# RWKV scan terms in four quarters of the PE array, and head sums in four column groups

## The chip, the cores and the metric

One core of a Trainium2 chip runs the whole kernel. The metric is device time in microseconds (us), the median of three runs. Everything is float32; matmuls are done either on float32 operands or on float32r operands, for which a value is split into a high and a low part and three products are summed.

## The reference, cut to what matters

The layer normalises and modulates 256 context and 2048 latent tokens of width 1024, projects them once, and feeds two groups of 8 heads of 64 channels: neighbourhood attention and a bidirectional RWKV-7 scan. Then come the output projection, a LayerNorm and a squared-ReLU MLP. The change touches the RWKV part alone:

```python
kk = split_heads(k * k_k, RW_HEADS)
kk = kk / jnp.maximum(jnp.sqrt(jnp.sum(jnp.square(kk), axis=-1, keepdims=True)), 1e-12)
kd = k[:, :, None] * (1 + (a - 1) * k_a)
...
s_kk = jnp.einsum('bhij,bhj->bhi', S, kk_t)
S = (S * w_t[:, :, None, :] - s_kk[..., None] * (kk_t * a_t)[:, :, None, :]
     + v_t[..., None] * k_t[:, :, None, :])
...
yn = _normalize(y, GN_EPS).reshape(B, T, RW_WIDTH) * gn_g + gn_b
```

So there are two sums over the 64 channels of a head, one of squared keys (for `kk`) and one of squared outputs (for `yn`). The scan is done in chunks of 64 tokens; inside a chunk it needs a 64x64 product of decayed keys with keys for each head, direction and chunk.

## The kernel before, in words

The instructions of each engine are put in order at build time: a scheduler walks the traced program, gives each engine the earliest instruction of the program whose inputs and buffers are ready by its own estimate, and fills gaps with later ones that are ready. The buffers of a tag are handed out in the order of the program.

**Phase 1** (about the first 1005 us) goes over three blocks of 768 tokens in 27 jobs each: the weight column block is loaded and split, `project` (L450) runs 24 matmuls into a PSUM bank, ScalarE copies the bank out (L453) and the job's own work follows. After each half of a job `side` runs one item of deferred work: the key norm, the scan terms, the transposes of values (`nav`, L726), and steps of the triangular solves.

`knorm` (L556) makes the key norm, in two halves of 384 tokens. For each of the four blocks `p` of 128 channels (two heads) it squares the keys (L564) and sums the channels of each head with a float32 matmul (L565) whose weights `hsel` have 8 columns; the four matmuls add into the same 8 rows of a PSUM bank. Square root, maximum and reciprocal follow on 8 rows, and `inv` holds the high part in rows 0 to 7 and the low part in rows 32 to 39 of a tile of 40 rows. `r1a` (L597) spreads it over 128 channels with a float32r matmul of 40 rows (L611).

`r1b` (L667) runs for each of 9 groups of 256 tokens and 4 channel blocks, 36 batches in all. It holds the 16 products of keys (L686): two directions `d`, four chunks `c`, two heads `hd`. Each takes 64 rows and 64 columns of the array, and head 0 uses the upper rows and left columns, head 1 the lower rows and right columns. All 16 go to one bank of the pool `psC`, which has two buffers that `nav`, the layer norm's transposes (L415) and the bonus matmul (L693) use too. One ScalarE copy (L688) and two DMA issues on ScalarE's queue (L690) write the products to the scratch `LB`, which the solves read (L733 on).

**The output stage** (about 1745 to 2090 us) runs beside the last eight steps of the scan's chain. For each 256 tokens `scales` (L1224) does for the outputs what `knorm` does for the keys (L1231 to L1238, tiles of the tag `hm`), and `readout` (L1240) loads `bo` and `gt` on SyncE's queue (L1247, L1249), spreads the scales (L1251) and multiplies. The output projection is L1346.

The chain's own products (`chain_pre`, L1141 and L1145; `chain_main`, L1173 and L1188) are not touched; they serve below as a pattern. L1141 uses the two quarters off the diagonal with 128 moving columns, L1145 the two on it with 64 columns, and they write two different banks.

Of the kernel before, what the change touches and what calls it, by code (L numbers as in the profile page):

```python
# [8 lines left out]
F32 = mybir.dt.float32  # L9
# [52 lines left out]
class Kern:  # L62
# [223 lines left out]
    def p1consts(self, k1):  # L286
# [23 lines left out]
        self.hsel = k1.tile([128, 4, 8], F32, name="hsel")  # L310
# [3 lines left out]
        self.hbc = k1.tile([40, 4, 128], F32R, name="hbc")  # L314
# [241 lines left out]
    def knorm(self):  # L556
        nc = self.nc
        inv = self.inv
        for h in range(2):
            s = slice(h * 384, h * 384 + 384)  # L560
            ps = self.psB.tile([128, 512], F32, name="psb")
            for p in range(4):
# [104 lines left out]
    def r1b(self, sb, p, t, v, cell):  # L667
# [556 lines left out]
    def scales(self, i):  # L1224
# [3 lines left out]
        psv = self.psO.tile([128, 512], F32, name="ops")[:, :256]  # L1228
        for p in range(4):
            sq = P.tile([128, 256], F32, tag="hm", name="ysq")  # L1230
            nc.scalar.activation(sq, y[:, p], AF.Square)  # L1231
            nc.tensor.matmul(psv[0:8], lhsT=self.hsel[:, p, :], rhs=sq, start=(p == 0), stop=(p == 3))
        x = P.tile([8, 256], F32, name="yinv", bufs=1)
        inv = self.inv[i % 2]
        nc.scalar.activation(x, psv[0:8], AF.Sqrt, scale=1.0 / 64, bias=self.eps[0:8, 1:2])
        nc.vector.reciprocal(x, x)
        nc.vector.tensor_copy(inv[0:8], x)
        nc.vector.tensor_tensor(inv[32:40], x, f32(inv[0:8]), ALU.subtract)  # L1238
# [23 lines left out]
    def out_init(self, es):  # L1262
# [9 lines left out]
        self.hsel = o1.tile([128, 4, 8], F32, name="hsel2")  # L1272
        nc.sync.dma_start(self.hsel, a["hsel"])
        hb = self.o2.tile([40, 4, 128], F32, tag="xres", name="hb2")
        nc.sync.dma_start(hb, a["hbc"])
        self.hbc = o1.tile([40, 4, 128], F32R, name="hbc2")
        nc.scalar.copy(self.hbc, hb)
        self.inv = [o1.tile([40, 256], F32R, name="inv%d" % i) for i in range(2)]
        for x in self.inv:
            nc.gpsimd.memset(f32(x), 0.0)  # L1280
# [579 lines left out]
def host(inputs):  # L1860
    I = {k: np.asarray(v) for k, v in inputs.items()}
    o = {}
# [70 lines left out]
```

## Time and profile before

| what | us |
|---|---|
| median of 3 runs | 3413.09 |
| lowest and highest run | 3408.29, 3415.94 |
| profiled execution, its own time | 3414.7 |
| its span | 3412.9 |

The profiled execution is one run of its own: 1.6 us over the median, and 1.8 us longer than the span that the trace covers. A fp32 matmul appears as two records (weights of a first and a second pass), a float32r one as one record; ends of matmuls are modelled, so the time that one takes on the engine is read from start to start.

### The profile page before, as it was taken

What the parts mean: (1) busy time and instruction counts of PE and PEld (TensorE: products, weight loads), DVE (VectorE), ACT (ScalarE), POOL (GpSimd) and SP (SyncE); (2) the same over time, 40 slices, a digit from 0 to 9 for tenths busy, and PEclk for the clock granted to TensorE, in tenths of its full rate; (3) what the DMA queues carried; (4) which work ended last, traced back from release to release, by engine and by line L of the source; (5) the groups of instructions that cost most, each with busy time, mean ns of one, the idle gap of its engine ahead of it and who ended that gap; (6) DMA issues with size and microseconds to landing.
All of it is one profiled execution on the core that took longest, in us unless ns stands there. A gap on an engine that the chain in (4) does not pass through costs nothing.

```text
span 3412.9 us, 65231 instructions
## 1 busy us (share of the span) xinstructions
PE 3192.8 (94%) x25176; PEld 2602.5 (76%) x25176; DVE 2599.1 (76%) x4907; ACT 1523.7 (45%) x2891; POOL 511.0 (15%) x535
## 2 busy tenths in 40 slices
PE   7999899899988899899979989999999989999998
PEld 3888888889876677677667767777788868888886
DVE  5567977888788778767768878866766657899778
ACT  4555465456535455454432124343433343337333
POOL 0000000000005454545343321000000000010001
PEclk9999999999989999999989989999999989999999
DMA  7487366826675655455374546666644455445441
GB/s 259 119 244 213 95 170 167 223 71 178 174 201 145 144 140 126 122 133 128 101 199 150 175 152 224 210 198 206 210 150 148 145 206 162 154 161 203 146 160 69
DMA packets 765338, 561.67 MB, mean 165 GB/s; under 512 B 380412, under 2 KB 653564, under 8 KB 763620
## 3 DMA queue, kind: packets, MB, share of 16 engines
q1 hardware_dynamic: 691738, 523.14, 52.0%
q10 hardware_dynamic: 73290, 34.37, 3.5%
q8 instruction: 198, 3.24, 0.4%
q14 instruction: 112, 0.92, 0.1%
HBM read 359.70 MB, written 197.66 MB: 163 GB/s over the span
## 4 chain that ended last, share of the span: by engine, by line
PE 65%; DVE 14%; DMA 11%; SPq 3%; issue 3%; ACT 2%; POOL 1%; ACTq 0%; DVEq 0%; POOLq 0%
PE psm L450 14%; PE psa L1530 8%; PE psqb L1728 7%; PE psqa L1728 7%; PE psb L1530 4%; PE ops L1346 4%; PE pse L1530 2%; PE psv L1051 2%; DMA ks<-AR 1%; PE psm L468 1%; DMA w<-in_mlp_w 1%; PE pst L1022 1%; PE psg L1141 1%; PE psl L986 1%; PE psd L117 1%
## 5 line engine op out<-in xcount | busy, mean ns | idle before, releaser
L450 PE MATMUL psm<-xh,wh 128*128 128x386 f32 (+1 forms) x1104 | 378.4, 345 | 17.4 <-DVE xh L420 9.5
L450 PE MATMUL psm<-xl,wh 128*128 128x386 f32 (+1 forms) x1104 | 378.8, 343 | 3.1 <-DVE xl L421 3.1
L450 PE MATMUL psm<-xh,wl 128*128 128x386 f32 (+1 forms) x1104 | 376.6, 341 | 0.0
L450 PEld LDWEIGHTS psm<-xh,wh 128*128 128x128 f32 x1104 | 209.2, 190 | 44.8 <-ACT row L453 15.1
L450 PEld LDWEIGHTS psm<-xl,wh 128*128 128x128 f32 x1104 | 209.5, 190 | 16.0 <-issue 8.0
L450 PEld LDWEIGHTS psm<-xh,wl 128*128 128x128 f32 x1104 | 208.8, 189 | 6.1 <-issue 4.1
L1530 PE MATMUL psa<-xh,w1h 128*128 128x512 f32 x512 | 203.9, 399 | 5.1 <-DVE p L1556 4.6
L1794 POOL TENSOR_TENSOR acc<-acc,g 128x1024 f32<-128x1024 f32 x8 | 28.9, 3641 | 1178.2 <-DVE acc L1737 1178.2
L1530 PE MATMUL psa<-xh,w1l 128*128 128x512 f32 x512 | 201.7, 394 | 2.5 <-DVE w1l L1461 2.5
L1530 PE MATMUL psa<-xl,w1h 128*128 128x512 f32 x512 | 202.3, 395 | 0.0
L1678 ACT CAST ah<-al 128x1024 fp32r<-128x1024 f32 x98 | 103.0, 1051 | 213.2 <-DMA al<-HU 205.1
L760 DVE TENSOR_TENSOR stmp<-mp,xp 128x1 f32<-128x1 f32 (+30 forms) x310 | 175.4, 566 | 22.7 <-DMA mp<-LB 10.3
L1679 DVE TENSOR_TENSOR al<-al,ah 128x1024 fp32r<-128x1024 f32 x98 | 121.3, 1237 | 86.0 <-ACT ah L1678 85.9
L436 DVE TENSOR_TENSOR wl<-wst,wh 128x1024 fp32r<-128x1024 f32 x81 | 98.8, 1220 | 98.5 <-ACT wh L435 85.8
L1461 ACT CAST w1h<-w1s 128x512 fp32r<-128x512 f32 x96 | 59.6, 621 | 226.4 <-DVE w1s L1450 87.4
L1728 PE MATMUL psqa<-uh,ah 128*128 128x512 f32 x400 | 155.8, 393 | 3.7 <-ACT uh L1634 3.2
L1728 PE MATMUL psqa<-ul,ah 128*128 128x512 f32 x400 | 157.4, 394 | 0.0
L1728 PE MATMUL psqa<-uh,al 128*128 128x512 f32 x400 | 157.0, 392 | 0.0
L1728 PE MATMUL psqb<-uh,ah 128*128 128x512 f32 x384 | 149.7, 393 | 7.5 <-ACT uh L1634 7.5
L761 DVE TENSOR_REDUCE xp<-stmp 128x1 f32<-128x1 f32 (+30 forms) x310 | 153.9, 497 | 3.1
L1728 PE MATMUL psqb<-ul,ah 128*128 128x512 f32 x384 | 151.0, 393 | 0.0
L1728 PE MATMUL psqb<-uh,al 128*128 128x512 f32 x384 | 150.6, 392 | 0.0
(393 smaller groups left out, 8816.2 us busy)
## 6 DMA issues: line engine op xcount, KB each, us to landing
al<-HU SPq DMA_DIRECT2D x106, 512.0 KB
wst<-in_w_in SPq DMA_DIRECT2D x81, 512.0 KB
w<-in_mlp_w SPq DMA_DIRECT2D x32, 1024.0 KB
wp<-in_mlp_w SPq DMA_DIRECT2D x32, 1024.0 KB
wmod<-in_w_mod SPq DMA_DIRECT2D x48, 512.0 KB
HU<-p SPq DMA_DIRECT2D x96, 256.0 KB
HU<-s SPq DMA_DIRECT2D x84, 256.0 KB
bkc<-BK SPq DMA_DIRECT2D x36, 512.0 KB
```

Source lines behind the costliest of these rows:

```text
L117: self.nc.tensor.matmul(acc[32 * j:32 * j + n, :], lhsT=self.sil[:, k, 0:n], rhs=w, start=(k == 0), stop=(k == 7))
L436: nc.vector.tensor_tensor(wl, w, f32(wh), ALU.subtract)
L450: nc.tensor.matmul(ps[:, :y - x], lhsT=s[:, k, :], rhs=m[:, k, x:y], start=(i == 0), stop=(i == 23))
L760: nc.vector.tensor_tensor(tv, mp[:, i:i + 1, lo:lo + n].to_broadcast([128, n, n]), xp[:, lo:lo + n, lo:lo + n], ALU.mult)
L761: nc.vector.tensor_reduce(xp[:, lo:lo + n, i], tv, AX.X, ALU.add)
L1051: nc.tensor.matmul(cell["ps"][hs, i0:i0 + n, :], lhsT=vt[:, hs], rhs=x, start=first, stop=last, skip_group_check=True)
L1346: nc.tensor.matmul(ps, lhsT=x[:, k, :], rhs=w[:, k, c], start=(i == 0), stop=(i == 23))
L1461: made[n] = nc.scalar.copy(h, x).ins, V.tensor_tensor(l, x, f32(h), ALU.subtract).ins
L1530: nc.tensor.matmul(ps, lhsT=w[:, k, :], rhs=x[:, k, :], start=(i == 0 and pr in (1, 5, 2)), stop=(i == 11), skip_group_check=True)
L1678: fs += [lambda: nc.scalar.copy(ah, f32(al)), fb[0], lambda: V.tensor_tensor(al, f32(al), f32(ah), ALU.subtract), fb[1]]
L1679: lambda: V.tensor_tensor(al, f32(al), f32(ah), ALU.subtract), fb[1]]
L1728: nc.tensor.matmul(ps, lhsT=x[:, c, s], rhs=y[:, c, :], start=(i == 0 and new), stop=(i == 5 and end), skip_group_check=True)
```

## The change

The sums over a head's channels go to four groups of 32 columns: block `p` writes rows 32p to 32p+31 of the bank, so the four matmuls no longer add into one another. `hsel` gets 32 columns, of which 4 are used (each head's sum twice), and `inv`, `hbc` and all that lies between get 128 rows, with the high part in two rows of each group, the low part in the next two, and zeros elsewhere. The squares are made first and the four matmuls follow; the second to fourth are pinned behind the one before. The products of keys are split into two banks, one for each direction; direction 1 writes head 0 to the lower and head 1 to the upper partitions, and the loop goes over chunks first, so that four matmuls in a row use the four quarters of the array. Two copies and three DMA issues replace one and two.

```diff
-        hb = self.r1.tile([40, 4, 128], F32, tag="bk", name="hb", bufs=2)
+        hb = self.r1.tile([128, 4, 128], F32, tag="bk", name="hb", bufs=2)
...
-        self.inv = k1.tile([40, 768], F32R, name="inv")
-        nc.gpsimd.memset(f32(self.inv), 0.0)
+        self.inv = k1.tile([128, 768], F32R, name="inv")
...
             for p in range(4):
-                sq = self.r1.tile([128, 384], F32, tag="hf", name="sq", bufs=3)
-                nc.scalar.activation(sq, self.ks[p][:, s], AF.Square, scale=self.vcol("k_k", p))
-                nc.tensor.matmul(ps[0:8, :384], lhsT=self.hsel[:, p, :], rhs=sq, start=(p == 0), stop=(p == 3))
-            x = self.r1.tile([8, 384], F32, tag="hf", name="kn", bufs=3)
-            nc.scalar.activation(x, ps[0:8, :384], AF.Sqrt)
+                sq.append(self.r1.tile([128, 384], F32, tag=("hf", "l2", "hf", "ta2")[p], name="sq", bufs=(3, 2)[p % 2]))
+                nc.scalar.activation(sq[p], self.ks[p][:, s], AF.Square, scale=self.vcol("k_k", p))
+            self.headsums(ps[:, :384], sq)
+            x = self.r1.tile([128, 384], F32, tag="hf", name="kn", bufs=3)
+            nc.scalar.activation(x, ps[:, :384], AF.Sqrt)
...
-            nc.vector.tensor_copy(inv[0:8, s], x)
-            nc.vector.tensor_tensor(inv[32:40, s], x, f32(inv[0:8, s]), ALU.subtract)
+            self.highlow(inv[:, s], x, self.r1.tile([128, 384], F32R, tag="hf", name="knh", bufs=3))
+
+    def headsums(self, ps, sq):
+        for p in range(4):
+            i = self.nc.tensor.matmul(ps[32 * p:32 * p + 32], lhsT=self.hsel[:, p, :], rhs=sq[p], start=True, stop=True)
+            if p:
+                self.tc.keep_in_program_order(i)
+
+    def highlow(self, dst, x, h):
+        nc = self.nc
+        nc.vector.tensor_copy(h, x)
+        nc.vector.tensor_scalar(x, x, self.vcol("hm", 0), None, ALU.mult)
+        nc.vector.scalar_tensor_tensor(dst, f32(h), self.vcol("hm", 1), x, ALU.mult, ALU.add)
...
-        psl = self.psC.tile([128, 512], F32, name="psc")
-        for d in range(2):
-            for c in range(4):
-                for hd in range(2):
-                    hs = slice(hd * 64, hd * 64 + 64)
-                    o = (d * 4 + c) * 64
-                    nc.tensor.matmul(psl[hs, o:o + 64], lhsT=bk[hs, d, c, 0, :], rhs=ar[hs, d, c, 0, :], start=True, stop=True)
-        lab = R.tile([128, 2, 4, 64], F32, tag="ei", name="lab")
-        nc.scalar.copy(lab.rearrange("p d c t -> p (d c t)"), psl)
-        for d in range(2):
-            nc.scalar.dma_start(self.LB[:, d, c0 * 4 + p:(c0 + 3) * 4 + p + 1:4, :], lab[:, d])
+        psl = [self.psC.tile([128, 4, 64], F32, name="psc") for _ in range(2)]
+        hs = [slice(0, 64), slice(64, 128)]
+        for c in range(4):
+            for d in range(2):
+                for h in range(2):
+                    nc.tensor.matmul(psl[d][hs[h ^ d], c, :], lhsT=bk[hs[h], d, c, 0, :], rhs=ar[hs[h], d, c, 0, :],
+                                     start=True, stop=True)
+        lab = R.tile([128, 2, 4, 64], F32, tag="ei", name="lab")
+        for d in range(2):
+            nc.scalar.copy(lab[:, d], psl[d])
+        lb = self.LB[:, :, c0 * 4 + p:(c0 + 3) * 4 + p + 1:4, :]
+        nc.scalar.dma_start(lb[:, 0], lab[:, 0])
+        for h in range(2):
+            nc.scalar.dma_start(lb[hs[h], 1], lab[hs[1 - h], 1])
```

In `scales` the same is done to tiles of 256 columns; the four squares take tags `hm`, `bo`, `hm`, `gt` (two buffers each, those of `readout`'s loads), and the high part takes `hm`. `out_init` loses two memsets on GpSimd and gets the wider `hsel`, `hbc` and `inv`.

## Rows read from the trace of the kernel before

**Rows 1.** The page, busy time of each engine: us, share, instructions.
```profile
PE 3192.8 (94%) x25176; PEld 2602.5 (76%) x25176; DVE 2599.1 (76%) x4907; ACT 1523.7 (45%) x2891; POOL 511.0 (15%) x535
```

**Rows 2.** Busy time by stretch: length, PE, PEld, DVE, ACT, POOL, clock, DMA.
```profile
100.00:1005.00 905.00, 864.69 (x6654) 766.59 (x6652) 706.35 (x1358) 485.11 (x879) 9.76 (x24) 0.98 0.63 168
...
1745.00:2090.00 345.00, 308.67 (x2674) 229.20 (x2670) 273.82 (x492) 91.35 (x205) 112.36 (x93) 0.92 0.57 177
```

**Rows 3.** The chain by line, phase 1 (100 to 1005 us), then the output stage.
```profile
by line: PE psm L450 49.8%; PE psm L468 5.2%; PE psc L686 3.3%; DMA xn<-in_x 2.4%; PE psb L614 2.0%; PE psb L565 2.0%; PE psd L117 1.9%; PE psb L624 1.7%; PE psb L582 1.6%; issue 1.5%; PE psb L628 1.5%; DMA LB<-lab 1.4%; PE psc L693 1.3%; D
...
by line: PE ops L1346 34.4%; issue 5.7%; DVE wo L1291 3.0%; DMA gt<-GT 2.9%; PE ops L1232 2.9%; PE ry L1202 2.5%; DMA bo<-BON 2.4%; PE ry L1184 2.4%; PE us L1188 2.3%; DVE yacc L1255 2.3%; DVE yl L1339 2.2%; DMA wo<-in_w_out 2.1%; PE psg L1
```

**Rows 4.** PE's timeline around one batch of L686: start, us, what; then L686's durations (ns).
```profile
608.79 1.15 PE L686 MATMUL psc<-ar,bk 64*64 64x64 f32 x32
609.87 0.50 PE L468 MATMUL psm<-xh,wh 128*128 128x512 f32 x1
...
L686 PE MATMUL psc<-ar,bk x1152: 218/218/365, 164.4 to 991.8; 64*64 64x64 f32 x192
```

**Rows 5.** Stretches of L1145 alone (first row), then of L1141 alone.
```profile
1297.80:1298.90 1.10, 0.82 (x16) 0.66 (x16) 1.00 0.37 102
...
1297.80:1298.90 1.10, 1.06 (x16) 0.85 (x16) 1.00 0.37 102
1303.00:1304.20 1.20, 1.09 (x16) 0.85 (x16) 1.00 0.43 167
```

**Rows 6.** PE's timeline, two groups of the chain.
```profile
1310.84 0.69 PE L1173 MATMUL ry<-SV,ks 128*64 128x64 f32 x16
...
1315.93 0.68 PE L1188 MATMUL us<-rh,xz 64*64 64x64 f32 x16
```

**Rows 7.** PE's timeline around one head sum.
```profile
404.42 0.34 PE L450 MATMUL psm<-xh,wl 128*128 128x386 f32 x1
404.69 0.81 PE L565 MATMUL psb<-sq,hsel 128*8 128x384 f32 x2
```

**Rows 8.** The chain in order of time, fourth and eighth head sum of that block.
```profile
430.88 0.74 PE psb L565 x2
...
443.86 0.74 PE psb L565 x2
```

**Rows 9.** PE's timeline around one spreading matmul L611.
```profile
169.16 0.28 PE L450 MATMUL psm<-xl,wh 128*128 128x258 f32 x1
169.27 0.28 PE L450 MATMUL psm<-xh,wl 128*128 128x258 f32 x1
169.48 0.38 PE L611 MATMUL psb<-inv,hbc 40*128 40x256 f32 x1
169.79 0.71 PE L614 MATMUL psb<-cmat,vx 128*128 128x128 f32 x4
```

**Rows 10.** ScalarE: issues, copies by group, one late copy in the timeline.
```profile
L690 ACTq DMA_DIRECT2D LB<-lab x72: 366/402/1500, 166.9 to 993.1; - x72
...
L688 ACT COPY lab<-psc 128x512 f32<-128x512 f32 x36 | 21.1, 585 | 41.1 <-PE psc L686 28.4 <-DVE bk L659 9.5 <-DVE rsw L715 3.1
...
613.53 0.59 ACT L688 COPY lab<-psc 128x512 f32<-128x512 f32 x1 [1.34 <-DVE bk L659]
```

**Rows 11.** Output stage, groups by line; then the chain in order of time, two head sums.
```profile
L1232 PE MATMUL ops<-ysq,hsel 128*8 128x256 f32 x64 | 19.0, 411 | 0.0
...
L1251 PE MATMUL ops<-inv,hbc 40*128 40x256 f32 x32 | 9.3, 378 | 6.2 <-DVE inv L1238 6.2
...
1872.05 0.96 PE ops L1232 x4
```

**Rows 12.** Timeline: squares of the second `scales`, and GpSimd's wait for `bo`.
```profile
1784.88 0.42 ACT L1231 ACTIVATE ysq<-yacc 128x256 f32<-128x256 f32 x1 [0.44 <-PE ops L1232]
...
1790.72 1.19 POOL L1254 TENSOR_TENSOR yacc<-yacc,bo 128x256 f32<-128x256 f32 x1 [1.74 <-DMA bo<-BON]
```

**Rows 13.** VectorE, one line: duration in ns, lowest, median, highest.
```profile
L568 DVE TENSOR_SCALAR kn<-kn x6: 341/348/350, 129.1 to 771.3; 8x384 f32<-8x384 f32 x6
```

More of the change, by code (lines that the diff above doesn't have):

```diff
@@ L308, in p1consts @@
         nc.vector.memset(self.smask.rearrange("p (c t) -> p c t", t=64)[:, :, 0:1], 0.0)
-        self.hsel = k1.tile([128, 4, 8], F32, name="hsel")
+        self.hsel = k1.tile([128, 4, 32], F32, name="hsel")
         nc.scalar.dma_start(self.hsel, a["hsel"])
-        hb = self.r1.tile([40, 4, 128], F32, tag="bk", name="hb", bufs=2)
+        hb = self.r1.tile([128, 4, 128], F32, tag="bk", name="hb", bufs=2)
         nc.scalar.dma_start(hb, a["hbc"])
-        self.hbc = k1.tile([40, 4, 128], F32R, name="hbc")
+        self.hbc = k1.tile([128, 4, 128], F32R, name="hbc")
         nc.scalar.copy(self.hbc, hb)
-        self.inv = k1.tile([40, 768], F32R, name="inv")
-        nc.gpsimd.memset(f32(self.inv), 0.0)
+        self.inv = k1.tile([128, 768], F32R, name="inv")
         v = self.vec
@@ L561, in knorm @@
             ps = self.psB.tile([128, 512], F32, name="psb")
+            sq = []
             for p in range(4):
-                sq = self.r1.tile([128, 384], F32, tag="hf", name="sq", bufs=3)
-                nc.scalar.activation(sq, self.ks[p][:, s], AF.Square, scale=self.vcol("k_k", p))
-                nc.tensor.matmul(ps[0:8, :384], lhsT=self.hsel[:, p, :], rhs=sq, start=(p == 0), stop=(p == 3))
-            x = self.r1.tile([8, 384], F32, tag="hf", name="kn", bufs=3)
-            nc.scalar.activation(x, ps[0:8, :384], AF.Sqrt)
+                sq.append(self.r1.tile([128, 384], F32, tag=("hf", "l2", "hf", "ta2")[p], name="sq", bufs=(3, 2)[p % 2]))
[3 more added lines that the diff above has]
+            nc.scalar.activation(x, ps[:, :384], AF.Sqrt)
             nc.vector.tensor_scalar(x, x, 1e-12, None, ALU.max)
             nc.vector.reciprocal(x, x)
-            nc.vector.tensor_copy(inv[0:8, s], x)
-            nc.vector.tensor_tensor(inv[32:40, s], x, f32(inv[0:8, s]), ALU.subtract)
+            self.highlow(inv[:, s], x, self.r1.tile([128, 384], F32R, tag="hf", name="knh", bufs=3))
[9 more added lines that the diff above has]
+        nc.vector.scalar_tensor_tensor(dst, f32(h), self.vcol("hm", 1), x, ALU.mult, ALU.add)
     def gate(self, sb, sg):
@@ L1228, in scales @@
         psv = self.psO.tile([128, 512], F32, name="ops")[:, :256]
+        sq = []
         for p in range(4):
[L1230 to L1235, printed above, removed]
+            sq.append(P.tile([128, 256], F32, tag=("hm", "bo", "hm", "gt")[p], name="ysq"))
+            nc.scalar.activation(sq[p], y[:, p], AF.Square)
+        self.headsums(psv, sq)
+        x = P.tile([128, 256], F32, name="yinv", bufs=1)
+        nc.scalar.activation(x, psv, AF.Sqrt, scale=1.0 / 64, bias=self.eps[:, 1:2])
         nc.vector.reciprocal(x, x)
-        nc.vector.tensor_copy(inv[0:8], x)
-        nc.vector.tensor_tensor(inv[32:40], x, f32(inv[0:8]), ALU.subtract)
+        self.highlow(self.inv[i % 2], x, P.tile([128, 256], F32R, tag="hm", name="yinvh"))
     def readout(self, i):
@@ L1271, in out_init @@
         self.l1g, self.l1b = l1
-        self.hsel = o1.tile([128, 4, 8], F32, name="hsel2")
+        self.hsel = o1.tile([128, 4, 32], F32, name="hsel2")
         nc.sync.dma_start(self.hsel, a["hsel"])
-        hb = self.o2.tile([40, 4, 128], F32, tag="xres", name="hb2")
+        hb = self.o2.tile([128, 4, 128], F32, tag="xres", name="hb2")
         nc.sync.dma_start(hb, a["hbc"])
-        self.hbc = o1.tile([40, 4, 128], F32R, name="hbc2")
+        self.hbc = o1.tile([128, 4, 128], F32R, name="hbc2")
         nc.scalar.copy(self.hbc, hb)
-        self.inv = [o1.tile([40, 256], F32R, name="inv%d" % i) for i in range(2)]
-        for x in self.inv:
-            nc.gpsimd.memset(f32(x), 0.0)
+        self.inv = [o1.tile([128, 256], F32R, name="inv%d" % i) for i in range(2)]
         g1 = self.o2.tile([128, D], F32, name="xn2", bufs=1)
@@ L1840 @@
 VLIST = [("c", 16), ("mu_prev", 15), ("mu_next", 15), ("w0", 8), ("a0", 8), ("k_k", 4), ("k_a", 4), ("r_k", 4),
-         ("gn_g", 4), ("gn_b", 4)]
+         ("gn_g", 4), ("gn_b", 4), ("hm", 2)]
 VOFF = {}
@@ L1866, in host @@
            "r_k": I["rw_r_k"], "gn_g": I["rw_gn_g"], "gn_b": I["rw_gn_b"]}
+    r = np.arange(128) % 32
+    src["hm"] = np.concatenate([r // 2 == 1, 1.0 * (r // 2 == 0) - (r // 2 == 1)]).astype(np.float32)
     for n, k in VLIST:
@@ L1878, in host @@
     o["bones"] = (hd[:, None] == hd[None, :]).astype(np.float32)
-    hs = np.zeros((128, 4, 8), np.float32)
-    hb = np.zeros((40, 4, 128), np.float32)
+    hs = np.zeros((128, 4, 32), np.float32)
+    hb = np.zeros((128, 4, 128), np.float32)
     for p in range(4):
-        for q in range(2):
-            hs[hd == q, p, 2 * p + q] = 1.0
-            hb[2 * p + q, p, hd == q] = 1.0
-            hb[32 + 2 * p + q, p, hd == q] = 1.0
+        for q in range(4):
+            hs[hd == q % 2, p, q] = 1.0
+            hb[32 * p + q, p, hd == q % 2] = 1.0
     o["hsel"], o["hbc"] = hs, hb
```

## The prediction

> **What bounds the kernel now.** I read the page first: TensorE (PE) is busy 94% of the span, and no other engine over 76% [rows 1]. The busy time by stretch shows where the edited lines lie: in phase 1 PE is busy 864.69 of 905 us beside 706.35 on VectorE and 485.11 on ScalarE; in the output stage 308.67 of 345, VectorE 273.82 [rows 2]. The chain says what ends last. In phase 1 its PE entries add up to about 80% of the stretch, L450 alone 49.8%; L686 has 3.3% and L565 2.0% [rows 3]. In the output stage PE entries make about half, L1232 2.9% of it, and waits for `bo` and `gt` another 5.3% [rows 3]. So PE time taken out of phase 1 should come back at about 0.8, in the output stage at about 0.5. The sum is made against the profiled execution's 3414.7 us, 1.6 us over the median of the runs.
>
> **A, the products of keys.** The reader should see in the timeline that a batch of 16 products is 32 records in 1.15 us, and that the next line starts 1.08 us after the first record [rows 4]. The last record is itself 0.218 us long [rows 4], so 32 starts spread over 0.93 us: 16 pairs, 62 ns for a pair, and two quarters already run side by side. Four at once would halve the spread: 0.46 us less. Can four run at once? The chain does it by accident: in the stretch from 1297.80 L1141 and L1145 run together, 16 records each, in 1.06 us; L1141 alone takes 1.09 us in another stretch [rows 5]. The 16 records of the other two quarters came free. They wrote another bank, as the change arranges it. The condition is that both banks are free at once, since buffers are what the scheduler waits for. Other groups use the same two buffers; I take 30 of 36 batches in quarters. The other 6 come out one direction after the other, and if other work slips between they pay one more switch of array shape. A switch is seen at L611: L450 follows L450 after 0.11 us, L611 after 0.21, and the next line comes 0.31 after L611, where a matmul of this length takes 0.11 [rows 9]. The two switches and weights that can't be loaded ahead cost 0.30 together; I take 0.25 for a split batch, whose weights are half as wide. Sum: 30 x 0.46 - 6 x 0.25 = 12.3 us of PE. Bounds: 36 x 0.46 = 16.6, and -9 if all are split.
>
> Behind it, on ScalarE: one copy of 0.585 becomes two of half the width, 0 to 0.585 more; and one issue more at 0.402 [rows 10]. I take 0.55 us, 20 us over 36 batches, under 485 us of work in 905, so it is hidden except where a solve waits for `LB`: "DMA LB" is 1.4% of the chain, 13 us [rows 3]. Six solves, each 0.55 later: 3 us lost, bounds 0 and 20. The bytes stay the same.
>
> **B, the spreading matmuls.** The reader sees a float32r matmul of 256 columns cost 0.52 us (from 169.27 to 169.79) where the two steps before and at it would take 0.22 without switches [rows 9]. With 128 rows L611 has the shape of its neighbours: 36 x 0.30 = 10.8 us less. Bounds: nothing, should the switch not come from the 40 rows, and 10.8. I take 10.4, as some neighbours are not of that shape. In the output stage 32 of the same take 9.3 us [rows 11]; at 0.11 each 3.5, so 6 less.
>
> **C, the sums for the key norm.** One insertion of L565 takes 0.74 us to the next line [rows 8], and 0.10 before it, since 0.27 us pass after a matmul that otherwise takes about 0.17 [rows 7]: 0.84 us. There are 24, eight in each block of tokens. Four at once would save 18 x 0.84 = 15 us. But the first half's four come at 404.69 and from there to 430.88, one after each block of keys [rows 7, 8]: each is placed when its own squares are ready. The pin holds the order of the four, not their closeness, and all but the last of the squares are ready as early as before. So I expect the first half to stay single and the second half (up to 443.86 [rows 8]), whose squares wait for buffers, to come in pairs: two insertions fewer a block, 6 x 0.84 = 5 us. Bounds 0 and 15.
>
> Three ops on VectorE replace two after the reciprocal: one multiplication more, 0.35 us by a `tensor_scalar` of the same width [rows 13], six times, and eight shorter ones in the output stage; 5 us at most, beside 706 us of work in 905 [rows 2]. Hidden by PE; uncovered it costs 5 us. The lost memsets on GpSimd and the larger tables, loaded twice, are ahead of need: 0 either way, at most 2 us.
>
> **D, the sums for the output norm.** Two matmuls in a row take 0.96 us [rows 11]; 32 take 19.0 us. Side by side in pairs 16 x 0.55 = 9, so 10 less; in fours 15; singly 0. But the squares now borrow buffers of `bo` and `gt`. Buffers of a tag go out in program order, so the squares of the second `scales`, at 1784.88 before, have to wait until the last `bo` and `gt` of the first `readout` have theirs, and that one's addition ran at 1790.72 after a wait for `bo` [rows 12]. I put 10 us of delay on that norm, of which the projection tiles in front of it hide part: 4 us lost, bounds 0 and 10. Behind the squares ScalarE holds the chain's copies; SyncE's loads of the next `readout` queue behind the squares, but come ten us early.
>
> **The sum.** Phase 1: 12.3 + 10.4 + 5 = 27.7 of PE, at 0.8 = 22, less 3 = 19. Output stage: (6 + 10) x 0.5 = 8, less 4 = 4. Together 23: 3414.7 - 23 = 3391.7 on the profile, and 1.6 less on the median: **3390**.
>
> A rule against A. On the chain L1173, whose column halves share all rows, does 16 records in 0.69 us, and L1188, whose two quarters share neither rows nor columns, does 16 in 0.68 [rows 6]. Weights that share rows cost no more there. The Trainium skill ("TensorE: Matmul & The Clock Gate", Part 3, The mechanism) says that weight loads overlap running matmuls only where their row groups differ. By it two quarters on the same rows would load in turn, A would give nothing, and the sum would be 3400. The rows speak against it, but not for four loads of 64 columns each at once, since L1141 streams twice as long.
>
> A second rule. L686's pairs come from different rows and write the same bank, and yet two records start every 62 ns [rows 4]. The Trainium skill ("TensorEngine Tiling (Array Packing)", Gotcha 1: PSUM Pressure) says that different row tiles cannot access one bank at the same time; by it A would gain nothing either, but the trace disagrees for pairs already.
>
> **The rivals.**
> - **Everything packs**: all 36 batches in quarters, the sums in fours, at the chain's share: (16.6 + 10.8 + 15) x 0.8 + (6 + 15) x 0.5 = 44.5, about 3370. For it: records that are ready together do run together [rows 4]. Against it: the four places of the first half [rows 7, 8].
> - **No gain from quarters**: weights sharing rows load in turn, A is 0: 3390 + 12.3 x 0.8 = 3400. For it: nothing shows four quarters at 64 columns. Against it: what A says of [rows 5, 6].
> - **It doesn't pack at all**: the two directions come apart and the sums stay single; the spreading matmuls alone gain, 10.4 x 0.8 + 3, against -9 x 0.8, 3 and 4 lost: about 3410, no measurable change. For it: the single places [rows 7, 8].
> - **Slower**: `psC`. A batch now holds both its buffers until its two copies are done. In the batch at 608.79 PE was through at 609.94 and the copy began only at 613.53 [rows 4, 10]: 3.6 us in which no transpose of L726 or L415 and no L693 could start. PE takes its instructions in a fixed order; if one of these stands next, L450 queues behind it and so do all who wait for `row`. It decides once the mean stall is over 23 / 36 = 0.64 us a batch; at 1.3 us it is 47 us lost, 23 won: 3437. Against it: ScalarE's wait at L688 is mostly for PE (28.4 of 41.1 us), so most copies follow at once [rows 10], and the order is laid out with buffers in mind.
>
> **How the numbers follow.** About 0.2%, 7 us, is what a measurement of this kernel can tell from no change. Chances: forecast 0.50, everything packs 0.20, no gain from quarters 0.10, no packing 0.10, slower 0.10. The forecast's own bounds (A from 0 to 16.6, C from 0 to 15, D's delay from 0 to 10) give 3376 to 3403. The range takes in the fully packed and the unpacked case, 3364 to 3411, and leaves out the slower one and a tail below. Faster by over 0.2%: nearly all of the forecast, everything packs, no gain from quarters and a part of no packing, 0.82; the same 0.09; slower 0.09.
>
> **What would show it.** A right: L686's 32 records spread over 0.5 us and the next line starts 0.6 us after the first; L686's share of phase 1's chain halves. B: L611 reads 128*128 and stands 0.12 us before its next line. C: fewer places with L565's successor, the first half still spread over 26 us. D: groups of four to eight records, and L1231's second group later than 1784.88. Wrong would be: quarters with records still 30 ns apart on average; PE idle before L726, L415 or L693 with ScalarE's copy as releaser; more VectorE waits for `LB`; or an output stage that gets longer.

## The result, and the profile of the changed kernel

The changed kernel takes 3433.56 us (median of four, 3427.79 to 3437.70) against 3410.69 for the kernel before on the same chip: ratio 1.0065, 95% interval 1.0046 to 1.0084. By that ratio it is 22 us slower (22.9 by the medians), where 23 us less was forecast. The profiled execution took 3437.7 us, its span is 3435.9.

The page, busy time of each engine and the chain by engine:

```profile
PE 3163.4 (92%) x25176; PEld 2594.0 (75%) x25176; DVE 2618.1 (76%) x4921; ACT 1516.6 (44%) x2925; POOL 513.4 (15%) x532
...
PE 55%; DVE 15%; DMA 10%; issue 4%; ACT 3%; SPq 3%; POOL 1%; ACTq 0%; DVEq 0%; POOLq 0%
```

Against [rows 1] TensorE is busy 29.4 us less, so the work did go away. But the span grew by 23.0 us, so TensorE is idle 52.4 us more (span less busy: 220.1 before, 272.5 now). That is the whole result in two numbers. The stretches of [rows 2], same columns, show it place by place:

```profile
100.00:1005.00 905.00, 839.98 (x6646) 755.47 (x6645) 704.80 (x1349) 482.89 (x914) 5.99 (x19) 0.96 0.64 166
1745.00:2090.00 345.00, 302.84 (x3153) 232.73 (x3150) 266.64 (x486) 89.67 (x208) 116.14 (x98) 0.90 0.56 174
```

In phase 1 TensorE does 24.7 us less in the same 905 us and does not get further: the last `project` matmul of phase 1 starts at 996.55 us before and at 1008.53 now (both rows below). The chain of phase 1, by line, answers to the first of [rows 3]:

```profile
by line: PE psm L450 28.2%; issue 4.1%; DMA LB<-lab 2.1%; DMA xn<-in_x 2.1%; PE psm L468 1.9%; DMA BK<-bk 1.9%; DVE wl L436 1.8%; DVE cum L653 1.7%; DVE xp L780 1.6%; PE psb L596 1.1%; DVE stmp L779 1.1%; DMA AR<-ar 1.1%; PE psb L819 1.0%; 
```

L450 falls from 49.8% to 28.2%, and waits of many kinds come up, none over 2.1%. All entries of TensorE together, small ones included, fall from 73.5% of the stretch to 36.4%: on this path phase 1 follows TensorE much less than before.

TensorE's groups for the edited lines (line, tile, count; then busy us and mean ns; then idle time before them), first those of before that [rows 11] don't have, then those of the change:

```profile
L686 PE MATMUL psc<-ar,bk 64*64 64x64 f32 x1152 | 43.6, 223 | 0.1
...
L614 PE MATMUL psb<-cmat,vx 128*128 128x128 f32 x144 | 25.6, 297 | 0.0
...
L565 PE MATMUL psb<-sq,hsel 128*8 128x384 f32 x48 | 19.5, 488 | 0.0
...
L611 PE MATMUL psb<-inv,hbc 40*128 40x256 f32 x36 | 13.7, 381 | 1.6 <-ACT l L631 1.6
```

```profile
L701 PE MATMUL psc<-ar,bk 64*64 64x64 f32 x1152 | 27.0, 230 | 13.1 <-DVE bk L670 13.1
...
L628 PE MATMUL psb<-cmat,vx 128*128 128x128 f32 x144 | 23.1, 283 | 0.0
...
L576 PE MATMUL psb<-sq,hsel 128*32 128x384 f32 x48 | 14.2, 498 | 0.0
...
L625 PE MATMUL psb<-inv,hbc 128*128 128x256 f32 x36 | 11.3, 313 | 6.5 <-ACT l L645 6.5
...
L1269 PE MATMUL ops<-inv,hbc 128*128 128x256 f32 x32 | 8.3, 338 | 5.6 <-DVE inv L585 4.7 <-DVE xres L1364 0.9
...
L576 PE MATMUL ops<-ysq,hsel 128*32 128x256 f32 x64 | 7.9, 431 | 2.7 <-DVE yacc L1270 2.7
```

A batch of products, now L701, to be read against [rows 4]:

```profile
556.69 0.34 PE L450 MATMUL psm<-xh,wl 128*128 128x386 f32 x1
556.86 0.33 PE L450 MATMUL psm<-xh,wh 128*128 128x386 f32 x1
557.13 0.69 PE L701 MATMUL psc<-ar,bk 64*64 64x64 f32 x32
```

32 records in 0.69 us instead of 1.15, and 27.0 us for all 36 batches against 43.6 before. Four quarters do run side by side. Now the waits of TensorE in phase 1 (line waited for, total us, times, longest):

```profile
PE psc L701 <- DVE bk L670: 13.1, 4, 6.3
...
PE psc L712 <- ACT lab L705: 7.8, 4, 2.0
...
PE psb L625 <- ACT l L645: 6.5, 2, 3.8
```

Before, L686 waited 0.1 us in all and L611 1.6. The second row is the wait that the rival "slower" named; it amounts to 7.8 us in four places.

### The profile page after: what moved, and what is told of

Read it like the earlier page. It is cut to its first block, busy times and chain, and to the rows that moved or that the text cites. A ratio compares the mean times of both kernels' runs of the same rounds, so it can differ in the third digit from the quotient of the medians.

```text
span 3435.9 us, 65328 instructions
## 1 busy us (share of the span) xinstructions
PE 3163.4 (92%) x25176; PEld 2594.0 (75%) x25176; DVE 2618.1 (76%) x4921; ACT 1516.6 (44%) x2925; POOL 513.4 (15%) x532
## 4 chain that ended last, share of the span: by engine, by line
PE 55%; DVE 15%; DMA 10%; issue 4%; ACT 3%; SPq 3%; POOL 1%; ACTq 0%; DVEq 0%; POOLq 0%
PE psa L1546 8%; PE psqa L1744 8%; PE psm L450 8%; PE psqb L1744 7%; PE psb L1546 4%; PE pse L1546 2%; PE psv L1070 2%; DMA ks<-AR 2%; DMA w<-in_mlp_w 1%; DMA qz<-Q 1%; PE psg L1160 1%; PE pst L1041 1%; PE psl L1005 1%; PE ops L1362 1%; PE psx L1008 1%
## 5 line engine op out<-in xcount | busy, mean ns | idle before, releaser
L450 PE MATMUL psm<-xh,wh 128*128 128x386 f32 (+1 forms) x1104 | 380.5, 347 | 14.4 <-ACT row L453 6.8
L450 PE MATMUL psm<-xl,wh 128*128 128x386 f32 (+1 forms) x1104 | 380.3, 345 | 3.6 <-DVE xl L421 3.5
L450 PE MATMUL psm<-xh,wl 128*128 128x386 f32 (+1 forms) x1104 | 378.3, 343 | 0.0
L450 PEld LDWEIGHTS psm<-xh,wh 128*128 128x128 f32 x1104 | 210.6, 191 | 38.5 <-ACT row L453 15.0
L450 PEld LDWEIGHTS psm<-xl,wh 128*128 128x128 f32 x1104 | 211.7, 192 | 14.0 <-DVE xl L421 7.1
L450 PEld LDWEIGHTS psm<-xh,wl 128*128 128x128 f32 x1104 | 210.7, 191 | 6.5 <-issue 5.1
L1744 PE MATMUL psqa<-uh,ah 128*128 128x512 f32 x400 | 155.5, 393 | 13.5 <-ACT uh L1650 13.5
```

The source lines that it names most:

```text
L450: nc.tensor.matmul(ps[:, :y - x], lhsT=s[:, k, :], rhs=m[:, k, x:y], start=(i == 0), stop=(i == 23))
L1744: nc.tensor.matmul(ps, lhsT=x[:, c, s], rhs=y[:, c, :], start=(i == 0 and new), stop=(i == 5 and end), skip_group_check=True)
```

## The experiments

Every one was timed in five rounds beside the kernel before on one chip. "Order" below means the order of each engine's instructions, which the scheduler lays when the program is built.

| kernel | us | ratio to before, 95% interval |
|---|---|---|
| the change | 3434 | 1.0065 (1.0046 to 1.0084) |
| e1, sums alone | 3420 | 1.0022 (1.0013 to 1.0032) |
| e15, sums alone, second order | 3407 | 0.9989 (0.9979 to 0.9999) |
| e14, sums without borrowed buffers | 3436 | 1.0081 (1.0065 to 1.0096) |
| e2, products alone | 3458 | 1.0133 (1.0117 to 1.0148) |
| e16, products alone, second order | 3447 | 1.0112 (1.0097 to 1.0127) |
| e6, before, heads swapped | 3437 | 1.0066 (1.0053 to 1.0080) |
| e12, before, stores swapped | 3437 | 1.0084 (1.0066 to 1.0102) |
| e11, the change, heads swapped | 3436 | 1.0076 (1.0057 to 1.0094) |
| e13, the change, directions swapped | 3433 | 1.0068 (1.0055 to 1.0081) |
| e9, before's order, spreading over 128 rows | **3396** | 0.9968 (0.9956 to 0.9980) |
| e10, the change's order, spreading over 40 rows | 3435 | 1.0077 (1.0059 to 1.0094) |

### Which half of the change? (e1, e2)

e1 is the change with the products as before, e2 the kernel before with the products in quarters.

```diff
 e1: the changed kernel
-        psl = [self.psC.tile([128, 4, 64], F32, name="psc") for _ in range(2)]
+        psl = self.psC.tile([128, 512], F32, name="psc")
...
 e2: the kernel before
-        psl = self.psC.tile([128, 512], F32, name="psc")
+        psl = [self.psC.tile([128, 4, 64], F32, name="psc") for _ in range(2)]
...
```

> The changed kernel with the products of keys as before (one bank, one copy, two DMA issues); the head sums and the 128-row spread stay changed. If the loss comes from the products' side (the tile lab shares the one buffer of ei, and a third DMA issue lands later; or both psC buffers are held), this is faster than before: PE has about 5 us less at the key sums, 6 us less at the spread in phase 1 and about 10 us less in the output stage, so 3395 to 3405 against 3411. If the loss comes from the sums (squares in l2, ta2, bo and gt), this is slower than before, 3420 to 3435. If any new order of the instructions costs tens of us, either way.

> The kernel before with the products of keys in four quarters (two banks, two copies, three DMA issues); the sums as before. If the loss comes from the products' side, it is here: 3425 to 3440, with ScalarE's ei waiting for the DMA of LB some 25 us in phase 1 (11 us before) and PE waiting for VectorE's bk. If it comes from the sums, this is faster than before by up to 13 us: 3398 to 3405.

e1 took 3420 us, e2 3458. Each half alone is slower than before, the products most, and the losses don't add up: 9 and 47 us for the halves, 22 for both. A cost that sits in one edit would add up, unless the orders of the three programs differ by as much. e2 lies above the 3425 to 3440 expected of it, and the `ei` wait for `LB` that was named as its cause is 13.2 us there, hardly more than before (next rows).

### A wait taken away (e3)

`lab` shares the single buffer of the tag `ei`, so the next `ei` waits until `LB` is stored. ScalarE's wait for it grew, before and after:

```profile
ACT ei L646 <- DMA LB<-lab: 11.3, 10, 3.0
```

```profile
ACT ei L660 <- DMA LB<-lab: 24.8, 18, 6.5
```

```diff
-        lab = R.tile([128, 2, 4, 64], F32, tag="ei", name="lab")
+        lab = R.tile([128, 2, 4, 64], F32, tag="l2", name="lab", bufs=2)
```

> The changed kernel with lab moved from the single buffer of ei to one of the two of l2. If the wait of ei for LB's DMA is the cause, ScalarE's wait for LB falls from 25 us to a few and the time falls to 3390 to 3405, below before. If the two held psC buffers are the cause, PE still waits at the bonus matmul for the copy (8 us after the change) and the time stays at 3425 to 3435. If it is the order as such, anything.

3435 us, 1.0079 (1.0063 to 1.0094): no change. The wait of `ei` for `LB` is gone. Other lines of ScalarE now wait for these stores, but less in all: 24.5 us, where all of its lines together waited 51.0 in the change and 16.7 before. TensorE's wait for the copy `lab` falls from 7.8 to 0.9 us, and others stand there (waits of TensorE in phase 1 of e3):

```profile
PE psc L701 <- DVE bk L670: 10.5, 2, 5.4
...
PE psc L712 <- DVE stmp L779: 7.5, 1, 7.5
```

So half of the waits for `LB` and nearly all of the stalls behind the copies went, and the time stayed. e3 is laid in an order of its own too, so this doesn't show what each wait is worth; it shows that taking away ScalarE's largest new wait did not give the time back.

### The same work in another order (e6, e12, e11, e13)

```diff
 e6: the kernel before
-                for hd in range(2):
+                for hd in (1, 0):
 e12: the kernel before, the two stores of a batch
-        for d in range(2):
+        for d in (1, 0):
             nc.scalar.dma_start(self.LB[:, d, c0 * 4 + p:(c0 + 3) * 4 + p + 1:4, :], lab[:, d])
```

> The kernel before with the two heads of each product of keys traced in the other order: the same instructions, the same buffers, the same work. It measures how much a re-laid order alone moves the time. If order as such is the cause, the time moves by 10 us or more; otherwise it stays within 7 us (0.2%) of before.

> The kernel before with the two stores of a product batch issued in the other order: same work, laid out anew from about a fifth of TensorE's rows on. If the time hangs on the laid order: more than 7 us from 3411, slower more probably than faster (3418 to 3440), as the swapped heads were. If the swapped heads were a single accident: 3406 to 3416.

Both took 3437 us: 26 and 29 us slower than the kernel before, with the same instructions, buffers and bytes. But both are laid anew: VectorE's instructions leave the order of before at about 250 us in e6 and at about 675 us in e12 (in e9, below, they never do). Where do they lose? Before and e12 end phase 1 together (last L450 at 996.55 and 996.12 us), but the chain's copy that starts at 2011.92 us before starts at 2044.73 in e12. So it is the stage between. A stretch of it (columns as in [rows 2]), before and in e12:

```profile
1500.00:1745.00 245.00, 226.49 (x3675) 179.76 (x3673) 176.32 (x521) 112.05 (x299) 102.25 (x119) 0.97 0.47 112
```

```profile
1500.00:1745.00 245.00, 220.44 (x3192) 173.66 (x3192) 173.80 (x507) 108.43 (x289) 96.69 (x111) 0.90 0.43 104
```

The third number from the end is the granted clock: 0.90 instead of 0.97. TensorE was busy almost as long and got through 3192 records instead of 3675 (not all the same ones, since e12 is behind). e6 shows the same, 0.90 and 3146. The page of e12 says the same of the whole:

```profile
PE 3205.8 (93%) x25176; PEld 2613.0 (76%) x25176; DVE 2611.0 (76%) x4907; ACT 1523.7 (44%) x2891; POOL 511.3 (15%) x535
```

13.0 us more busy time than before for the same 25176 records, and 15.2 us more idle (3441.1 - 3205.8 against 220.1). So this order costs twice: the waits themselves, and work that takes longer at a lower clock.

The change was given other orders in the same way: e11 swaps `h`, e13 swaps `d`.

```diff
 e11: the changed kernel
-                for h in range(2):
+                for h in (1, 0):
 e13: the changed kernel
-            for d in range(2):
+            for d in (1, 0):
```

> The changed kernel with the two heads of a product batch issued in the other order: same instructions, same buffers, but the order of the whole program is laid out anew. If the time hangs on the laid order, it lies elsewhere in a band of some 30 us, more than 7 us from 3434, on either side, and TensorE's work in phase 1 stays at 840 us. If the change's own waits (key tiles late, two held buffers) cost the time, they are still there: 3427 to 3441.

> The changed kernel with the two directions of a product batch issued in the other order: a third order of the same work (the first two took 3434 and 3436 us). If any new order costs the kernel some 25 to 30 us against the order of before, as three did that change no work: 3425 to 3445. If the orders scatter widely, it can be anywhere from 3400 to 3460, and the difference between the kernels was chance.

3436 and 3433 us. Three orders of the change lie within 3 us of one another, and so do two new orders of the kernel before, at the same place. The order of before is better than its other two by 26 to 29 us; compared with these the change gains nothing that could be measured.

The totals agree, but the places of the loss don't. Start of the last `project` matmul (L450) of phase 1, and of the 31st and 50th copy of the chain, us:

| kernel | last L450 | 31st copy | 50th copy |
|---|---|---|---|
| before | 996.55 | 1413.60 | 1665.35 |
| e6 | 997.48 | 1420.72 | 1698.78 |
| e12 | 996.12 | 1426.62 | 1698.27 |
| the change | 1008.53 | 1438.60 | 1690.03 |
| e11 | 1004.77 | 1428.08 | 1695.88 |
| e13 | 1008.30 | 1444.50 | 1703.35 |

The new orders of before end phase 1 level with it and lose 26 and 20 us between the 31st and the 50th copy. Every order of the change ends phase 1 late, by 8 to 12 us, although TensorE's busy time there is 22 to 26 us less. One wait of TensorE, 13.1 us in the change (above), comes back in each of them, in e11 and in e13:

```profile
PE psc L701 <- DVE bk L670: 14.8, 4, 7.9
```

```profile
PE psc L701 <- DVE bk L670: 18.0, 4, 8.0
```

Before and e6 have no such row, e12 has 1.6 us. So part of what the change loses in phase 1 comes back in each of its three orders. The expectation of e11 put 3427 to 3441 us down to the change's own waits, and its 3436 lies there; that the change loses by its order alone is not shown.

### One edit in an unchanged order (e9, e10)

e9 reads 128 rows in the spreading matmuls and adds no instruction: table and zeros lie in one tile, which one memset clears.

```diff
-        self.hbc = k1.tile([40, 4, 128], F32R, name="hbc")
-        nc.scalar.copy(self.hbc, hb)
-        self.inv = k1.tile([40, 768], F32R, name="inv")
-        nc.gpsimd.memset(f32(self.inv), 0.0)
+        hi = k1.tile([128, 1280], F32R, name="inv")
+        self.hbc, self.inv = hi[:, 768:].rearrange("p (a b) -> p a b", a=4), hi[:, :768]
+        nc.gpsimd.memset(f32(hi), 0.0)
+        nc.scalar.copy(self.hbc[0:40], hb)
...
 the same for the two tiles of the output stage
```

> The kernel before, in which the spreading matmuls (key norm and output norm) read 128 rows instead of 40, the added rows zero; zeros and table lie in one tile, so that no instruction is added and every engine keeps the order of the kernel before, row by row. So this is the term B of the prediction alone, without a re-laid order. If local savings come back at the shares of the chain (0.8 of 10.8 us, 0.5 of 6 us): 11 to 12 us faster, about 3399. If savings on TensorE are swallowed by waits even in an unchanged order: 3409 to 3412. If the switch does not come from the rows, L611 keeps its 0.31 us and the time is 3411.

3396.36 us, 10.9 us faster (0.9968 of 3408.58; interval 7 to 15): the forecast for B alone, and **the fastest kernel of this case**. TensorE's timeline around one L611, to be read against [rows 9]:

```profile
166.18 0.28 PE L450 MATMUL psm<-xh,wl 128*128 128x258 f32 x1
166.29 0.28 PE L611 MATMUL psb<-inv 128*128 128x256 f32 x1
166.41 0.61 PE L614 MATMUL psb<-cmat,vx 128*128 128x128 f32 x4
```

L611 follows after 0.11 us and its successor after 0.12: 0.23 us where 0.52 stood. The Trainium skill ("TensorEngine Tiling (Array Packing)", Key Properties) says that a change of tiling mode drains the engine; the trace fits this, at 0.29 us for one matmul of 40 rows between others of 128. The last L450 of phase 1, before and e9:

```profile
996.55 0.33 PE L450 MATMUL psm<-xh,wl 128*128 128x386 f32 x1
```

```profile
983.03 0.33 PE L450 MATMUL psm<-xh,wl 128*128 128x386 f32 x1
```

13.5 us earlier, more than the 36 x 0.29 = 10.4 of these matmuls, so a single execution has a few us of its own. Nothing of it is lost later: the copy of the chain that starts at 2011.92 before starts at 1996.95.

e10 is the counterpart: the changed kernel in its own order, row by row, with 40 rows.

```diff
-        nc.tensor.matmul(psk[:, :256], lhsT=self.hbc[:, p, :], rhs=self.inv[:, s], start=True, stop=True)
+        nc.tensor.matmul(psk[:, :256], lhsT=self.hbc[0:40, p, :], rhs=self.inv[0:40, s], start=True, stop=True)
```

> The changed kernel, in which the spreading matmuls read 40 of the 128 rows (the rows from 40 on are left out of the sums); every engine keeps the order of the changed kernel, row by row. If term B is worth in this order what the trace of the changed kernel shows on TensorE (L625 5.8 us and L1269 2.1 us shorter than before): 4 to 12 us slower than the changed kernel, 3438 to 3446. If the waits of the new order swallow it: 3431 to 3437.

3435 us, the same as the change. Why, the trace tells. The last L450 of phase 1, in the change and in e10:

```profile
1008.53 0.33 PE L450 MATMUL psm<-xh,wl 128*128 128x386 f32 x1
```

```profile
1019.41 0.33 PE L450 MATMUL psm<-xh,wl 128*128 128x386 f32 x1
```

10.9 us apart: in phase 1 term B is worth in this order what it is worth in the other. Then the 12th, 31st and 68th copy of the chain, in the change and in e10:

```profile
1165.79 0.37 ACT L1194 COPY rh<-ry 128x256 f32<-128x256 f32 x1 [0.76 <-PE ry L1192]
...
1438.60 0.37 ACT L1194 COPY rh<-ry 128x256 f32<-128x256 f32 x1 [0.78 <-PE ry L1192]
...
1990.38 0.37 ACT L1194 COPY rh<-ry 128x256 f32<-128x256 f32 x1 [0.31 <-PE ry L1192]
```

```profile
1178.21 0.37 ACT L1194 COPY rh<-ry 128x256 f32<-128x256 f32 x1 [0.76 <-PE ry L1192]
...
1443.90 0.38 ACT L1194 COPY rh<-ry 128x256 f32<-128x256 f32 x1
...
1990.81 0.37 ACT L1194 COPY rh<-ry 128x256 f32<-128x256 f32 x1 [0.51 <-PE ry L1192]
```

12.4 us apart, then 5.3, then 0.4. The saving is lost between 1166 and 1990 us, in steps of 2 to 4 us. A part is waits: TensorE stands 25.4 us for the loads `ks` of the chain (L1160) in the change and 22.1 in e10: the program that comes earlier waits longer. Another part is the clock (the stretch from 1500 to 1780, the change, then e10):

```profile
1500.00:1780.00 280.00, 253.88 (x4041) 199.62 (x4040) 195.19 (x567) 125.96 (x339) 114.43 (x133) 0.95 0.49 118
```

```profile
1500.00:1780.00 280.00, 254.31 (x4092) 200.67 (x4090) 197.06 (x583) 130.54 (x352) 118.20 (x138) 0.97 0.50 120
```

0.95 against 0.97, and 51 records more for the same busy time. That the waits swallow it was the second of the two expectations. The times alone leave room (e10 is 1 us slower than the change by the medians, by the ratios 4 us, 9 us either way); it is the traces that show nothing left at the 68th copy. So one and the same edit is worth 11 us in the one order and nothing that could be measured in the other.

### More orders of the halves (e14, e15, e16)

e15 and e16 are e1 and e2 with the heads of a batch swapped. e14 has the sums of the change on the kernel before, without the borrowed tags, the pins and the third VectorE operation:

```diff
-            nc.vector.tensor_copy(inv[0:8, s], x)
-            nc.vector.tensor_tensor(inv[32:40, s], x, f32(inv[0:8, s]), ALU.subtract)
+            nc.vector.tensor_copy(inv[:, s], x)
+            nc.vector.scalar_tensor_tensor(inv[:, s], f32(inv[:, s]), self.vcol("hm", 0), x, ALU.mult, ALU.add)
```

> The kernel before with both kinds of sums as the change has them (four column groups, spreading over 128 rows) but without its side effects: squares stay in their own buffers, two VectorE operations instead of three, nothing pinned; products as before. Terms B, C and D, about 11 + 4 + 5 = 20 us of saving, in a new order. If a new order costs 25 to 30 us by itself: 3411 to 3422, like the sums alone (3420). If the sums alone lost by the borrowed buffers and the third operation: 3390 to 3400.

> The change's sums with the products of before, the heads of a batch swapped: a second order of the kernel that took 3420 us. If a new order costs 25 to 30 us and the sums give 17 back: 3415 to 3425 again. If orders scatter widely: more than 7 us from 3420.

> The products in quarters alone, with the heads of a batch swapped: a second order of the kernel that took 3458 us. If the products cost by their own waits (two held buffers, an issue and a copy more), some 20 us over any new order of before (3437): 3450 to 3465 again. If 3458 was one bad order: 3415 to 3445.

e15 took 3407 us, 13 less than e1, outside the 3415 to 3425 expected; e14 took 3436, more than any expectation; e16 3447, below its band by 3. Within one kind of kernel orders lie up to 13 us apart here. The milder form of the sums came out worst, which gives no sign that the borrowed buffers or the third operation cost; as it is one order, it doesn't rule it out.

### Buffers, stores and quarters (e17 to e22)

Do the products cost by what they hold? e17 has two buffers, two half copies and two stores without quarters, e21 is e17 with the heads swapped, e18 is e2 with one bank from `psB`, e19 is e2 with two stores, e20 the kernel before with three, e22 the change without quarters (its stores don't exchange the heads).

```diff
 e17, e22: e2 and the change
-                    nc.tensor.matmul(psl[d][hs[h ^ d], c, :], lhsT=bk[hs[h], d, c, 0, :], rhs=ar[hs[h], d, c, 0, :],
+                    nc.tensor.matmul(psl[d][hs[h], c, :], lhsT=bk[hs[h], d, c, 0, :], rhs=ar[hs[h], d, c, 0, :],
 e18: e2
-        psl = [self.psC.tile([128, 4, 64], F32, name="psc") for _ in range(2)]
+        psl = [self.psC.tile([128, 4, 64], F32, name="psc"), self.psB.tile([128, 4, 64], F32, name="psb")]
 e19: e2
-        for h in range(2):
-            nc.scalar.dma_start(lb[hs[h], 1], lab[hs[1 - h], 1])
+        nc.scalar.dma_start(lb[:, 1], lab[:, 1])
```

> The kernel before, each batch of products in two buffers of psC with two half copies, but no heads exchanged: pairs as before, two issues as before. If holding both buffers is what costs: 3447 to 3465, like the products in quarters or worse, since the 16 us of TensorE are not saved. If it costs nothing beyond a new order: 3430 to 3444.

> The products in quarters alone, the second direction's bank taken from psB, so that a batch holds one buffer of psC. If holding both buffers of psC is what costs: 3415 to 3435, the 16 us now won against a new order of before (3437). If not: 3445 to 3460, as in the two orders before.

> The products in quarters alone, with one store for the second direction instead of two (its heads are left exchanged in what is stored). If the third issue of 0.4 us a batch is what costs: 3415 to 3435. If not: 3445 to 3460.

> The kernel before with three stores a batch instead of two, products as before. A new order alone: 3430 to 3444. If the third issue costs: 3447 to 3465.

> Two buffers of psC and two half copies a batch, pairs as before, the heads of a batch swapped: a second order of the kernel that took 3469 us. If the two buffers cost about 30 us beyond a new order (3437): 3460 to 3478. If the first order was a bad one: 3425 to 3450.

> The whole change, but both directions write the same quarters, so that they run in pairs again; buffers, copies and stores as in the change. If the quarters are worth the 16 us that they save on TensorE: 3444 to 3456. If they are worth nothing in a program that waits elsewhere: 3430 to 3440.

| kernel | us | ratio to before, 95% interval |
|---|---|---|
| e17 | 3469 | 1.0168 (1.0148 to 1.0189) |
| e21 | 3438 | 1.0077 (1.0064 to 1.0090) |
| e18 | 3503 | 1.0251 (1.0227 to 1.0275) |
| e19 | 3439 | 1.0077 (1.0062 to 1.0092) |
| e20 | 3420 | 1.0028 (1.0014 to 1.0041) |
| e22 | 3452 | 1.0126 (1.0104 to 1.0149) |

Against the expectations, e17 and e18 came out above every band, e20 below both, e19 between its two; e21 fits a bad first order, e22 the worth of the quarters. e17 seemed to show that two held buffers cost 30 us; e21, the same in a second order, took 30 us less, at the place of e6 and e12, so 30 us are not their price. A smaller cost in phase 1 stays likely: with two banks of `psC` the last L450 starts at 1008 to 1013 us in e2, e16, e17, e21 and e22 (1000.28 in e19), with one bank at 996 to 1003 in e6, e12, e14, e15 and e20 (1009.60 in e1). e18 shows what a really scarce buffer looks like: TensorE waits 46.0 us for key tiles in phase 1, one wait of 13.6.

e20 gives no sign that the third store costs: at 3420 it lies below the two new orders with two. It also shows that a new order of before need not cost 26 us; this one costs 9. e19, with one store less, lies 7 and 18 us under the two orders of e2, but e20 speaks against the store as the reason. e22 puts the pairs back into the change:

```profile
L701 PE MATMUL psc<-ar,bk 64*64 64x64 f32 x1152 | 43.7, 226 | 14.4 <-DVE bk L670 14.1
```

16.7 us more on TensorE than the 27.0 of the change, and about 19 us more time, though in another order.

## Why the prediction was wrong, point by point

**A, the products.** The mechanism was right, the size at the upper bound: 43.6 - 27.0 = 16.6 us, 35 of 36 batches at the pace of quarters, and one, at 292.64 us, in two parts of 16 records at the pace of pairs. The rule of the Trainium skill weighed there ("TensorE: Matmul & The Clock Gate", Part 3, The mechanism), by which two quarters on the same rows load in turn, didn't hold: 32 records in 0.69 us. One reading was wrong: "DMA LB" in the chain was put down to the solves; nearly all of it (10.4 of 12.8 us on the path) led to ScalarE's `ei`, which shares a buffer with `lab`. That wait doubled, and in e3, without it, the time was the same.

**B, the spreading matmuls.** Right in phase 1 (0.29 us at the one shown; 10.9 us of the whole program in e9, where 11 to 12 were expected). In the output stage 6 us were counted, and the records gave 1.0 (9.3 to 8.3).

**C and D, the sums.** Right: 19.5 to 14.2 us where 5 were forecast, and 19.0 to 7.9 where 10 were. In C the packing came as forecast as well, the first half single (two records are one matmul), the second in pairs (four records):

```profile
120.22 0.83 PE L576 MATMUL psb<-sq,hsel 128*32 128x384 f32 x2
...
141.27 0.84 PE L576 MATMUL psb<-sq,hsel 128*32 128x384 f32 x4
```

A pair takes the time of a single one. Over the three blocks there are seven pairs, six of them in second halves, where six were forecast.

The delay by borrowed buffers is there, but small: one wait of 3.5 us of the squares for `gt`, while GpSimd's waits for `bo` fell from 13.3 to 8.3 us.

**The sum is the step that failed.** The terms on TensorE were 12.3 + 10.4 + 5 + 16 = 43.7 us; the groups show 16.6 + 5.9 + 5.3 + 11.1 = 38.9 (5.9 for B: 2.4 on L611, 2.5 on its successor L614, 1.0 on L1251), of which the page shows 29.4 over all lines; the other lines got 9.5 longer, at a mean clock of 0.959 instead of 0.968. They were multiplied by 0.8 and 0.5, the shares of TensorE in the chain of before (its entries in phase 1 add up to 73.5%, not to 80, a matter of 2 us), and a program laid anew had no price. The runs show in its place that TensorE's work fell and its idle time rose by more, 52.4 us: phase 1 was to end 19 us earlier and ended 12.0 later, and in its other two orders 8.2 and 11.8 later. In the order of before the sum held for B: e9 gave 10.9 us where 10.4 x 0.8 + 6 x 0.5 = 11.3, though the 6 weren't there. In the order of the change, e10 shows, what B saves in phase 1 is lost in the chain stage.

A share of the chain is a weak factor in any case, since it is read from one path of one execution: L450 has 28.2% of phase 1 in the change and 35.1% in e10, which has the same order, and in e9, followed back from the end, the path never reaches phase 1. How much of the 22 us is the price of a new order and how much the change's own waits is not shown. Swaps that change no work cost 26 to 29 us in all, but not in phase 1, where the change is already 12.0 us behind.

**The rivals.** None was this one. "Slower" named 3437 us, close to the result, but by stalls behind `psC`'s two buffers: TensorE waited 7.8 us for the copies where 47 were needed, and e3 lost all but 0.9 of these and stayed. Its number was right by luck; that two held banks cost less than that in phase 1 is not ruled out. Two sums of the prediction are off: "no packing" is 11.3 won against 14.2 lost, so about 3416 and not 3410, and the forecast's own upper bound, with D's delay at 10 us, is 3410 and not 3403. The result lies above both. The part before the result says that a scheduler lays the order by its own estimate; that the order could come out worse as a whole was a rival to be priced, and it was left out.

**Open.** What makes the order of before the best of the three orders of that work isn't settled: the loss is spread over many waits of a few us and a lower clock in the chain stage. Nor is it settled why TensorE waits for `bk` in the change: it does so for 10.5 to 18.0 us in all six programs with both halves (also e3, e10 and e22), and for at most 4.1 in those with one half or with two banks alone, e18 left out. Nor is the worth of the quarters in a new order: e2, e16 and e19 (3439 to 3458) lie above e6 and e12, e22 against the change says the opposite, and orders of one kind lie up to 30 us apart. Neither A, C nor D could be tried in the order of before; their edits changed it each time.

## What to carry to other kernels

Where a scheduler lays the program, an edit has two effects, its own and that of the new order, and the second can use up the first: here 26 to 29 us (0.7 to 0.8%) for two swaps that change no work, against 38.9 us saved on TensorE. Equal totals don't show an equal cause; comparing when each program reaches the same point, as in the table above, showed two different places. So time a few neutral orders of both kernels before an edit is judged, and make the edit first in a form that leaves the order as it is, as e9 does: what it then gives is its own. A share of the chain may turn saved work into time as long as the order holds; where the edit changes the order, it is no forecast.

## What was not expected of the hardware

Idle time cost TensorE more than itself here. In the changed kernel it waits 4.91 us for ScalarE at 317.95 us; its timeline, and the stretches before the wait, behind it, and around a batch of products much later (columns as in [rows 2]):

```profile
317.95 0.69 PE L450 MATMUL psm<-xh,wh 128*128 128x386 f32 x1 [4.91 <-ACT row L453]
318.44 0.53 PE L450 MATMUL psm<-xl,wh 128*128 128x386 f32 x1
318.76 0.53 PE L450 MATMUL psm<-xh,wl 128*128 128x386 f32 x1
```

```profile
305.00:313.00 8.00, 7.63 (x75) 7.03 (x73) 8.00 (x20) 4.36 (x10) 0.00 (x0) 1.00 0.87 253
317.90:321.00 3.10, 3.05 (x9) 3.05 (x10) 2.58 (x9) 1.04 (x3) 0.00 (x0) 0.50 0.85 221
894.90:896.30 1.40, 1.13 (x32) 0.94 (x32) 1.40 (x4) 0.00 (x0) 0.00 (x0) 0.50 0.98 152
```

Matmuls that start every 0.17 us at full clock (556.69 and 556.86 above) start every 0.32 here; the granted clock is 0.50, the lower of its two levels (1.2 GHz), and was 1.00 before the wait. The batch of products that comes after a wait of 6.28 us takes 1.13 us at 0.50 instead of 0.69, and so loses almost all that the quarters save:

```profile
895.06 1.13 PE L701 MATMUL psc<-ar,bk 64*64 64x64 f32 x32 [6.28 <-DVE bk L670]
```

Four quarters of 64 columns at once, two of them on the same rows, cost no more here than two: 16 pairs took 0.93 us of starts before, 8 groups of four take 0.47 (0.69 less the last record's 0.22).
